# Mixer: values stored in runs of 512 bytes, first head's values loaded in the first pair, residual loaded behind the branches

## The chip, the cores and the metric

The kernel runs on one core of a Trainium2 chip. A core has TensorE (PE, matrix products), VectorE (DVE), ScalarE (ACT) and GpSimd (POOL) for element-wise work, SyncE (SP) that issues transfers, and DMA engines that move data between HBM and the on-chip memories SBUF (128 partitions) and PSUM (eight banks, where TensorE writes). Transfers are issued from SP, from ScalarE and from GpSimd; an issue stands in its engine's own order. The metric is the time of one execution in microseconds (us) on the device.

## What is computed

One layer of an encoder block on 1024 tokens of 1024 features, in float32. The part that matters here is the token mixer between two feed-forward networks:

```python
h = h + 0.5 * swiglu(rms_norm(h, ffn1_norm), ...)
u = rms_norm(h, mix_norm)
z = u @ w_in
q, k, v, s_in, gates = jnp.split(z, splits, axis=-1)          # 512, 512, 512, 512, 2048 columns
y_attn = neighbourhood_attention(q, k, v, na_rpb) @ w_attn_out  # 8 heads of 64, 16 x 64 token grid, window 8 x 16
y_ssm = s5_branch(s_in, ...) @ w_ssm_out                        # forward and backward scans of complex states, gated unit
g_attn, g_ssm = jnp.split(jax.nn.sigmoid(gates), 2, axis=-1)
h = h + (g_attn * y_attn + g_ssm * y_ssm) @ w_out
h = h + 0.5 * swiglu(rms_norm(h, ffn2_norm), ...)
...
```

The neighbourhood attention reads, for each query, keys and values of a window of 8 grid rows by 16 grid columns, adds a learned bias per head, and takes a softmax. The state-space branch scans the sequence in both directions, adds a skip term, and passes through a gated unit.

## The kernel before

Features lie on partitions, tokens along the free dimension, in two halves `t` of 512 tokens (`HT`). The normalised input of the mixer is held on chip in blocks of 128 features (`U`). Each product is done with operands split into a high and a low part, as three matmuls (`mm3`, lines 188 to 192), so that a weight block is first cast on ScalarE (`wh`, line 159) and its rest taken on VectorE (`wl`, line 160). The big products use a scheme with seven block products for a two-by-two matrix of blocks (`A7`, `ACC7`), with sums and differences of blocks made on VectorE.

The mixer has two streams of work on TensorE. The **main stream** makes the branch input (`proj`, lines 1415 to 1426), the values (`values(t)`, line 1427), and then twelve pairs of output blocks (`pairs`, line 1487: four of queries and keys, eight of gates), seven items each (`s_run`, line 1544). The weight blocks of an item are loaded from ScalarE's queue (`s_load`, line 1499) and cast some items ahead (`s_ahead`). The **side stream** is a generator (`mixer_side`, line 1312) that is advanced by `tick()`, called after every three matmuls of the main stream; a `yield n` in it means that it goes on n ticks later. In this order it does:

- `u_second`, the second half of the norm;
- sixteen injections (`inject`, line 1128): products of the branch input with small matrices, whose loads (`inject_load`, two of `fmi` and two of `ut` a pair, all from SP) run three pairs ahead; the results go into the buffer `X`;
- the scan, 128 steps on GpSimd (`scan_steps`), spread over what follows;
- attention in 64 units (8 heads, 2 row halves, 4 column blocks): scores (`attn_scores`), transposes two units later (`attn_turn`, line 1246), products with the values four units later (`attn_values`). Keys, queries, values and bias tables come from SP: `load_k` (L1203), `load_q` (L1210), `load_v` (L1215), `load_tab` (L1222). The unit order waits, as the program is written, until the first pair of query and key blocks is stored (`ready`);
- the state-space output (`ssm_out`) and the gated unit (`glu_load`, `glu_half`, lines 1272 to 1307).

Queries, keys, values, gates and both branches go through HBM, because attention reads windows of them in another layout. The values are kept as `v_d`, one row of 512 numbers for each head and grid place: four token groups of high part (64) and low part (64). `values(t)` copies each of four banks into `vh` (ScalarE) and takes `vl` (VectorE), and stores each at once from ScalarE's queue (L1449); one store writes, for 128 tokens, 64 numbers (256 bytes) into each of eight heads. The residual `h` is read back after the mixer (L1607) by sixteen loads of 256 KB from SP, into the place where `X` was.

Around it, `load_br` (lines 1451 to 1473) loads both branches, and `branches`, `gates` and `gated` multiply them with their output weights and with the gates, in four rounds of two feature blocks; `out_run` then adds the output product to the residual (L1694).

The order on TensorE is that of the program (a block of manual order). The order on the other engines is made by a planner: among the instructions that are ready by its own estimate of durations, each engine takes the one that stands first in the program; a block marked `high_priority` counts as standing 300 places earlier. Later instructions are thus put forward where an engine is free. Buffers of one tag are handed out in turn; work tiles `tmp` and weights `w` of the mixer share one tag of 24 buffers.

Of the kernel before, what the change touches and what calls it, by code (L numbers as in the profile page):

```python
# [8 lines left out]
F32 = mybir.dt.float32  # L9
# [3 lines left out]
ALU = mybir.AluOpType  # L13
# [28 lines left out]
def encoder_block(ctx, tc, I, out):  # L42
# [41 lines left out]
    def tmp(name, shape=(P, HT), dt=F32):  # L84
        return at("tmp", shape, dt, name)
# [1036 lines left out]
    def inject_load(pr):  # L1122
        fm = [ta("fmi", [P, 256]) for _ in range(2)]
        for d in range(2):
            nc.sync.dma_start(fm[d], f_d[pr, :, d * 256:(d + 1) * 256])
        return load_u(pr), fm

    def inject(pr, ut, fm):
# [62 lines left out]


    vdr = v_d.rearrange("h (r c) d -> h r c d", r=4)
    vds = v_d.rearrange("h p (g a d) -> p g a h d", g=4, a=2)
    khl, qs, vld, tabs = {}, {}, {}, {}
    late = []
    halves2 = slice(0, 64), slice(64, P)
# [114 lines left out]
    def mixer_side():  # L1312
        yield from u_second()
        while 3 not in stored:
            yield 1
        yield 7
        new_x()
        ld = {}
        for pr in range(3):
            ld[pr] = inject_load(pr)  # L1320
        yield 10
        for pr in range(NPAIR):
            if pr + 3 < NPAIR:
                ld[pr + 3] = inject_load(pr + 3)
            inject(pr, *ld.pop(pr))
            yield 2
        while 0 not in ready:
            scan_steps(1)
            yield 1
        units = [(hd, rb, cb) for hd in range(NH) for rb in range(2) for cb in range(4)]  # L1330
        n = len(units)
        load_tab(0, 0)
        load_k(0)
        load_q(0, 0)
        for cb in range(4):
            load_v(0, cb)
        for _ in range(6):
            scan_steps(1)
            yield 2
        sms, pts, O = {}, {}, {}  # L1340
        late.clear()
        lo, so = {}, {}
        for j in range(n + 5):
            if j < n:
                hd, rb, cb = units[j]
                b = 2 * hd + rb
                load_tab(b + cb // 2, (1, 2, 0, 0)[cb]) if cb < 3 else None
                if cb == 1 and rb == 0:
                    load_q(hd, 1)
                if cb == 1 and rb == 1 and hd + 1 < NH:  # L1350
                    while hd + 1 not in ready:
                        yield 1
                    load_q(hd + 1, 0)
                if rb == 0 and cb == 2 and hd + 1 in ready:
                    load_k(hd + 1)
                if rb == 1 and cb == 2 and hd + 1 < NH and hd + 1 not in khl:
                    load_k(hd + 1)
                sms[j] = attn_scores(hd, rb, cb)
            if 0 <= j - 2 < n:
                pts[j - 2] = attn_turn(units[j - 2][2], sms.pop(j - 2))  # L1360
            while late:
                nc.scalar.dma_start(*late.pop())
            if 0 <= j - 4 < n:
                hd, rb, cb = units[j - 4]
                if cb == 0:
                    O[hd, rb] = bank("O")
                attn_values(hd, rb, cb, O[hd, rb], *pts.pop(j - 4))
                if rb == 1 and hd + 1 < NH:
                    load_v(hd + 1, cb)
            scan_steps(2)  # L1370
            if j >= n:
                if j - n < 3:
                    lo[j - n] = ssm_load(j - n)
            yield 3
        scan_steps(NCH)
        for p in range(NPAIR + 1):
            if 3 <= p + 3 < NPAIR:
                lo[p + 3] = ssm_load(p + 3)
            if p < NPAIR:
                so[p] = ssm_out(p, *lo.pop(p))  # L1380
            if p > 0:
                so.pop(p - 1)()
            yield 1 + p % 2
        yield 3
        glu_load(0)
        raws = [glu_raw(0), glu_raw(1)]
        yield 11
        glu_act(0)
        glu_load(1)
        yield 2  # L1390
        glu_act(1)
        for t in range(2):
            yield from glu_half(t, raws)
# [33 lines left out]
    def values(t):  # L1427
        os_ = [bank("v") for _ in range(4)]
        for k in range(NK):
            load_wv()  # L1430
            if t == 1 and k == 0:
                s_ahead(-2)
            if t == 1 and k == 5:
                s_ahead(0)
            wh, wl = Wv[k]
            xs = U[("a11", "a12", "a21", "a22")[2 * t + k // 4]][k % 4]
            for i in range(4):
                xh, xl = (x[:, ksl(i)] for x in xs)
                T.matmul(os_[i], lhsT=xh, rhs=wh, start=(k == 0), stop=False)
                T.matmul(os_[i], lhsT=xh, rhs=wl, start=False, stop=False)  # L1440
                T.matmul(os_[i], lhsT=xl, rhs=wh, start=False, stop=(k == NK - 1))
                tick()
        for i in range(4):
            vh, vl = tmp("vh", dt=F32R), tmp("vl", dt=F32R)
            with tc.high_priority(offset=PRI):
                A.copy(vh, os_[i])
                V.tensor_tensor(vl, os_[i], vh.bitcast(F32), ALU.subtract)
            for j, x in enumerate((vh, vl)):
                nc.scalar.dma_start(vds[ksl(i % 2), 2 * t + i // 2, j], x.rearrange("p (h d) -> p h d", h=NH).bitcast(F32))  # L1449

    def load_br(t, b):

        res = []
        if b == 0:
            for k in range(0, 4, 2):
                st = tst("br")
                nc.sync.dma_start(st.rearrange("p (k c) -> p k c", k=2),
                                  o_d[k * P:(k + 2) * P, hsl(t)].rearrange("(k p) c -> p k c", p=P))
                for i in range(2):
                    hi, lo = tx("bh"), tx("bl")  # L1460
                    split(hi, lo, st[:, hsl(i)])
                    res.append((hi, lo))
            return res
        for k in range(4):
            st = tmp("br")
            hi, lo = tx("bh"), tx("bl")
            nc.sync.dma_start(st.rearrange("p (s c) -> p s c", s=L),
                              y2_d[ksl(k)].rearrange("p (s c) -> p s c", s=L)[:, :, t * 64:(t + 1) * 64])
            sv = st.rearrange("p (s c) -> p c s", s=L)
            hv, lv = (x.rearrange("p (c s) -> p c s", s=L) for x in (hi, lo))  # L1470
            split(hv, lv, sv)
            res.append((hi, lo))
        return res
# [96 lines left out]

    for t in range(2):
        values(t)
    s3s = []
    for k in range(4):
        s3 = tmp("s3")
# [26 lines left out]
    lp = ctx.enter_context(tc.tile_pool(name="lt", bufs=1, reuse_waits="tile"))  # L1602
    cur.update(tmp=(lp, "m", 17), w=(lp, "w", 20))
    h = new_h()
    for t in range(2):
        for j in range(NK):
            nc.sync.dma_start(h[j][t], h_d[:, (2 * j + t) * HT:(2 * j + t + 1) * HT])  # L1607


    def h2_block(j, t):  # L1610
# [337 lines left out]
```

## Time and profile before

| | |
|---|---|
| timed runs | 2 (2122.85 and 2125.08 us), median 2123.97 us |
| profiled execution | 2116.88 us |
| its span, first to last instruction | 2115.1 us |
| mean granted TensorE clock | 0.994 |
| TensorE busy | 2059.3 us (97%) |
| VectorE, ScalarE, GpSimd busy | 1458.8, 1010.1, 437.9 us |
| DMA packets under 512 bytes | 53472 of 225521 |

The profile is of one execution. Busy times leave out the issuing of transfers: a row with `ACTq` or `SPq` is such an issue, standing in the order of ScalarE or SP. A time in brackets is how long the engine had been idle before the row, and what ended that. "Waits" list who waited for whom; a wait for several things is put down to the one that came last. The chain of waits is followed back from the last instruction to what released each step. Some matmul records are missing from a trace, so counts in a short stretch can be a little low.

The mixer lies between about 690 and 1345 us of the span: values of the second token half and injections up to 790, the first items and the first attention units from 790 to 850, attention to 1065, state-space output to 1117, gated unit to 1172, branches from 1196 on.

### The profile page before, as it was taken

The page shows a single profiled execution, that of the slowest core. Times are in us where ns is not written, and L with a number is a line of the kernel's source. Part 1 is how long each engine was busy: PE and PEld are TensorE (multiplying, and loading weights), DVE is VectorE, ACT ScalarE, POOL GpSimd, SP SyncE. Part 2 cuts the span into 40 slices and gives each one's busy share as a digit, 9 for nine tenths or more (in the row PEclk, how much of TensorE's full clock was granted, in tenths as well). Part 3 has the DMA queues.
Part 4 walks back from the last instruction along what each step waited for, and adds up shares of the span by engine and source line. Part 5 has one row for each costly group of instructions (what it writes and reads, how often), then busy time and mean ns, then how long its engine had stood idle before and what let it go on. Part 6 is the DMA issues. An engine that isn't in the chain of part 4 may idle for free.

```text
span 2115.1 us, 28193 instructions
## 1 busy us (share of the span) xinstructions
PE 2059.3 (97%) x9518; PEld 1680.8 (79%) x9518; DVE 1458.8 (69%) x2470; ACT 1010.1 (48%) x1870; POOL 437.9 (21%) x656
## 2 busy tenths in 40 slices
PE   8999999999999997999988999999999999999998
PEld 3788888888888885788876788788888888888887
DVE  7897776667967745677644669896566565785855
ACT  6434333344445434677645546553333334545544
POOL 0037555540000518888000002000000000000000
PEclk9999999999999999999999999999999999999999
DMA  3434444485533466667677757142423338533302
GB/s 131 142 119 152 127 131 131 137 283 157 183 118 112 143 167 206 194 213 217 184 230 258 231 179 172 65 154 90 135 80 119 101 100 286 171 111 95 114 27 80
DMA packets 225521, 319.74 MB, mean 151 GB/s; under 512 B 53472, under 2 KB 93024, under 8 KB 225376
## 3 DMA queue, kind: packets, MB, share of 16 engines
q1 hardware_dynamic: 180752, 268.62, 40.0%
q10 hardware_dynamic: 42000, 44.07, 6.5%
q0 software_dynamic: 2624, 5.24, 1.3%
q8 instruction: 75, 1.23, 0.2%
q14 instruction: 70, 0.57, 0.1%
HBM read 224.01 MB, written 93.85 MB: 150 GB/s over the span
## 4 chain that ended last, share of the span: by engine, by line
PE 82%; DMA 7%; DVE 6%; ACT 2%; issue 1%; SPq 1%; ACTq 0%; DVEq 0%
PE dx L190 4%; PE dx L191 4%; PE dx L192 4%; PE gx L190 3%; PE ux L190 3%; PE gx L191 3%; PE ux L192 3%; PE ux L191 3%; PE gx L192 3%; PE dy L192 2%; PE dy L190 2%; PE dy L191 2%; PE gy L190 2%; PE uy L190 2%; PE uy L192 2%; PE gy L192 2%
## 5 line engine op out<-in xcount | busy, mean ns | idle before, releaser
L159 ACT CAST wh<-hbuf 128x512 fp32r<-128x512 f32 x280 | 172.8, 622 | 390.2 <-PE gx L191 83.5
L160 DVE TENSOR_TENSOR wl<-hbuf,wh 128x512 fp32r<-128x512 f32 x280 | 210.0, 753 | 123.9 <-ACT wh L159 121.7
L159 ACT CAST wh<-wblk 128x512 fp32r<-128x512 f32 x190 | 118.0, 622 | 193.6 <-PE dx L191 82.4
L160 DVE TENSOR_TENSOR wl<-wblk,wh 128x512 fp32r<-128x512 f32 x190 | 130.7, 690 | 50.4 <-ACT wh L159 42.9
L190 PE MATMUL dx<-ah,wh 128*128 128x512 f32 x416 | 163.5, 393 | 0.4 <-DVE hbuf L694 0.3
L192 PE MATMUL dx<-ah,wl 128*128 128x512 f32 x416 | 161.9, 389 | 0.0
L191 PE MATMUL dx<-al,wh 128*128 128x512 f32 x416 | 161.9, 389 | 0.0
L160 DVE TENSOR_TENSOR al<-araw,ah 128x512 fp32r<-128x512 f32 x154 | 106.3, 694 | 49.1 <-PE dx L191 21.1
L190 PE MATMUL gx<-xh,wh 128*128 128x512 f32 x320 | 124.9, 390 | 1.2 <-DVE c L581 1.2
L190 PE MATMUL ux<-xh,wh 128*128 128x512 f32 x320 | 124.9, 390 | 0.0
L191 PE MATMUL gx<-xl,wh 128*128 128x512 f32 x320 | 124.5, 389 | 0.0
L192 PE MATMUL ux<-xh,wl 128*128 128x512 f32 x320 | 124.5, 389 | 0.0
L192 PE MATMUL gx<-xh,wl 128*128 128x512 f32 x320 | 124.5, 389 | 0.0
L191 PE MATMUL ux<-xl,wh 128*128 128x512 f32 x320 | 124.5, 389 | 0.0
L159 ACT CAST ah<-araw 128x512 fp32r<-128x512 f32 x154 | 95.0, 619 | 43.8 <-PE dx L191 14.2
L160 DVE TENSOR_TENSOR wl<-blk,wh 128x512 fp32r<-128x512 f32 x84 | 60.8, 727 | 70.1 <-ACT wh L159 69.7
L190 PEld LDWEIGHTS dx<-ah,wh 128*128 128x128 f32 x416 | 78.1, 188 | 18.6 <-DVE hbuf L694 1.2
L428 DVE TENSOR_TENSOR hbuf<-hbuf 128x512 f32<-128x512 f32 x120 | 90.4, 754 | 2.8 <-DMA hbuf<-in_wu 0.7
L191 PEld LDWEIGHTS dx<-al,wh 128*128 128x128 f32 x416 | 78.1, 188 | 16.7 <-issue 0.7
L1156 POOL TENSOR_TENSOR sc<-X,rho 128x128 f32<-128x128 f32 x128 | 78.5, 613 | 61.6 <-ACT X L1139 51.6
L192 PEld LDWEIGHTS dx<-ah,wl 128*128 128x128 f32 x416 | 78.1, 188 | 16.3
L190 PE MATMUL px<-xh,wh 128*128 128x512 f32 x192 | 79.2, 412 | 4.3 <-ACT z L1532 3.4
(397 smaller groups left out, 5713.2 us busy)
## 6 DMA issues: line engine op xcount, KB each, us to landing
araw<-a_d SPq DMA_DIRECT2D x154, 256.0 KB
a_d<-c SPq DMA_DIRECT2D x148, 256.0 KB
wblk<-in_wd SPq DMA_DIRECT2D x88, 256.0 KB
hbuf<-in_wg SPq DMA_DIRECT2D x40, 512.0 KB
hbuf<-in_wu SPq DMA_DIRECT2D x40, 512.0 KB
blk<-in_win ACTq DMA_DIRECT2D x48, 256.0 KB
hbuf<-in_xT SPq DMA_DIRECT2D x32, 256.0 KB
h_d<-hbuf ACTq DMA_DIRECT2D x32, 256.0 KB
```

Of the source, the lines that this page charges most:

```text
L159: A.copy(hi, src)
L160: return eng.tensor_tensor(lo, src, hi.bitcast(F32), ALU.subtract)
L190: T.matmul(o, lhsT=wh, rhs=xh, start=first, stop=False, skip_group_check=more)
L191: T.matmul(o, lhsT=wh, rhs=xl, start=False, stop=False, skip_group_check=more)
L192: T.matmul(o, lhsT=wl, rhs=xh, start=False, stop=last, skip_group_check=more)
L428: V.tensor_tensor(b11, (b12, b22, None, None, b21)[i - 2], b11, ALU.subtract)
L1156: G.tensor_tensor(sc, both, rho4, ALU.mult)
```

## The change

There are four edits.

1. **Layout and stores of the values.** The rows of `v_d` are now four groups of 128 numbers, high and low part side by side as before, and a store covers both: `vs` holds, for four heads, high and low parts together. One store writes 512 bytes into each of four heads; there are again eight stores for a half, of 512 runs each instead of 1024. The copies and subtractions work on 256 columns each. The stores are not issued at once but put into the list `later`, which `s_store()` empties: for the first half in the third step of the second half's `values`, for the second half after it.
2. **Injection loads.** The second `fmi` load of a pair is issued from ScalarE instead of SP.
3. **Values of the first head.** `load_v(0, cb)` and the first table stand in the side stream right after the injections and after the last store of values, with four scan steps and four ticks before each, instead of behind the first keys and queries.
4. **Residual.** The sixteen loads of `h` are ordered behind the last load of a branch on SP.

```diff
     def inject_load(pr):
         fm = [ta("fmi", [P, 256]) for _ in range(2)]
         for d in range(2):
-            nc.sync.dma_start(fm[d], f_d[pr, :, d * 256:(d + 1) * 256])
+            (nc.sync, nc.scalar)[d].dma_start(fm[d], f_d[pr, :, d * 256:(d + 1) * 256])
         return load_u(pr), fm
...
-    vds = v_d.rearrange("h p (g a d) -> p g a h d", g=4, a=2)
+    vds = v_d.rearrange("h p (g d) -> p g h d", g=4)
...
             inject(pr, *ld.pop(pr))
             yield 2
+        while "v" not in stored:
+            scan_steps(1)
+            yield 1
+        for cb in range(4):
+            scan_steps(4)
+            yield 4
+            load_v(0, cb)
+        load_tab(0, 0)
         while 0 not in ready:
             scan_steps(1)
             yield 1
         units = [(hd, rb, cb) for hd in range(NH) for rb in range(2) for cb in range(4)]
         n = len(units)
-        load_tab(0, 0)
         load_k(0)
         load_q(0, 0)
-        for cb in range(4):
-            load_v(0, cb)
...
             if t == 1 and k == 0:
                 s_ahead(-2)
+            if t == 1 and k == 2:
+                s_store()
             if t == 1 and k == 5:
                 s_ahead(0)
...
         for i in range(4):
-            vh, vl = tmp("vh", dt=F32R), tmp("vl", dt=F32R)
-            with tc.high_priority(offset=PRI):
-                A.copy(vh, os_[i])
-                V.tensor_tensor(vl, os_[i], vh.bitcast(F32), ALU.subtract)
-            for j, x in enumerate((vh, vl)):
-                nc.scalar.dma_start(vds[ksl(i % 2), 2 * t + i // 2, j], x.rearrange("p (h d) -> p h d", h=NH).bitcast(F32))
+            for q in range(2):
+                vs = tmp("vs", [P, 4, 2, 64], F32R)
+                ov = os_[i][:, q * 256:(q + 1) * 256].rearrange("p (h d) -> p h d", h=4)
+                with tc.high_priority(offset=PRI):
+                    A.copy(vs[:, :, 0], ov)
+                    V.tensor_tensor(vs[:, :, 1], ov, vs[:, :, 0].bitcast(F32), ALU.subtract)
+                later.append((nc.scalar, vds[ksl(i % 2), 2 * t + i // 2, 4 * q:4 * q + 4],
+                              vs.rearrange("p h a d -> p h (a d)").bitcast(F32)))
...
-            nc.sync.dma_start(st.rearrange("p (s c) -> p s c", s=L),
-                              y2_d[ksl(k)].rearrange("p (s c) -> p s c", s=L)[:, :, t * 64:(t + 1) * 64])
+            mark["br"] = nc.sync.dma_start(st.rearrange("p (s c) -> p s c", s=L),
+                                           y2_d[ksl(k)].rearrange("p (s c) -> p s c", s=L)[:, :, t * 64:(t + 1) * 64]).ins
...
     for t in range(2):
         values(t)
+    s_store()
+    stored.add("v")
...
-    for t in range(2):
-        for j in range(NK):
-            nc.sync.dma_start(h[j][t], h_d[:, (2 * j + t) * HT:(2 * j + t + 1) * HT])
+    with tc.issue_after(mark["br"]):
+        for t in range(2):
+            for j in range(NK):
+                nc.sync.dma_start(h[j][t], h_d[:, (2 * j + t) * HT:(2 * j + t + 1) * HT])
```

## The prediction

> **What bounds the kernel now.** I read the head of the page first, then the waits of TensorE (engine, line, whom it waited for: total us, times, longest us).
>
> ```profile
> span 2115.1 us, 28193 instructions
> PE 2059.3 (97%) x9518; PEld 1680.8 (79%) x9518; DVE 1458.8 (69%) x2470; ACT 1010.1 (48%) x1870; POOL 437.9 (21%) x656
> ```
>
> ```profile
> PE pt L1246 <- ACT sm L1239: 15.0, 7, 7.5
> PE px L190 <- ACT z L1532: 3.4, 2, 3.2
> PE glu L190 <- ACT yh L159: 3.0, 2, 2.4
> PE inj L1132 <- DMA ut<-u_d: 2.5, 2, 2.0
> ```
>
> TensorE is busy for 2059.3 of 2115.1 us, so all its idle time is 55.8 us. The change takes no matmul away; it can only win from those 55.8 us and from matmuls that run slowly after a pause. Next I asked the timeline of TensorE for the places (start, us, line; in brackets the idle time before it and what ended it), and the chain of waits for the pace of the matmuls behind each pause (start, us, what).
>
> ```profile
> 771.61 1.32 PE L1132 MATMUL inj<-ut,fmi 128*128 128x128 f32 x8 [2.05 <-DMA ut<-u_d]
> 799.56 0.50 PE L190 MATMUL px<-xh,wh 128*128 128x512 f32 x1 [3.19 <-ACT z L1532]
> 845.97 0.90 PE L1246 MATMUL pt<-ident,sm 128*128 128x128 f32 x3 [7.49 <-ACT sm L1239]
> 1139.30 0.51 PE L190 MATMUL glu<-yh,wgl 128*128 128x512 f32 x1 [2.37 <-ACT yh L159]
> ```
>
> ```profile
> 801.98 0.43 PE px L191
> 847.72 0.43 PE px L192
> 1141.03 0.23 PE glu L190
> ```
>
> After the pauses of 3.19 and 7.49 us a 512-column matmul takes 0.43 us, after 2.37 us it takes 0.23. The twelve matmuls from 799.56 end at 804.1 instead of 802.4: 1.8 us more. Behind 845.97 about seven are slow: 1.6 us. So four places hold what the change can reach: **A**, the injections (2.5 us); **B**, the first branch products behind the values (3.19 + 1.8 = 5.0); **C**, the first attention units (7.49 + 1.6 = 9.1); **D**, the gated unit behind the scan. D comes from the windows (stretch, its length, PE busy, ..., DMA share, GB/s): PE is idle for 3.87 and 1.60 us, together 5.5.
>
> ```profile
> 1130.00:1140.00 10.00, 6.13 (x22) 3.97 (x22) 3.85 (x7) 3.52 (x8) 0.00 (x0) 1.00 1.05 395
> 1140.00:1150.00 10.00, 8.40 (x34) 6.32 (x35) 5.66 (x10) 5.28 (x10) 0.00 (x0) 1.00 0.61 207
> 1190.00:1200.00 10.00, 9.49 (x41) 7.34 (x40) 5.24 (x7) 5.97 (x8) 0.00 (x0) 1.00 0.77 207
> ```
>
> A + B + C + D = 22.1 us is the most that the change can win.
>
> What holds these places is ScalarE, and what holds ScalarE is a transfer. Its timeline, then the chain of waits at the same places:
>
> ```profile
> 762.27 0.37 ACT L1139 COPY X<-inj 64x256 f32<-64x256 f32 x1 [3.31 <-issue]
> 788.93 0.59 ACT L1446 CAST vh<-v 128x512 fp32r<-128x512 f32 x1 [7.23 <-PE v L1441]
> 797.25 1.11 ACTq L1449 DMA_DIRECT2D v_d<-vl  x1
> 798.40 0.62 ACT L159 CAST wh<-blk 128x512 fp32r<-128x512 f32 x1 [5.26 <-DMA v_d<-vh]
> 842.33 0.62 ACT L159 CAST wh<-blk 128x512 fp32r<-128x512 f32 x1 [6.95 <-DMA k_d<-qkh]
> 1138.11 0.62 ACT L159 CAST wh<-blk 128x512 fp32r<-128x512 f32 x1 [6.48 <-DMA hbuf<-h_d]
> ```
>
> ```profile
> 763.18 5.64 DMA v_d<-vl
> 768.89 2.58 DMA ut<-u_d
> 827.43 14.39 DMA vhl<-v_d
> 841.89 0.34 ACTq L1499
> 1132.25 5.36 DMA hbuf<-h_d
> 1137.71 0.35 ACTq L1499
> ```
>
> The issue on ScalarE at 841.89 loads a weight block and reads nothing of the values, yet it goes out when the value load of 827.43 has landed; so does the one at 1137.71 behind a load of the residual. So an issue here waits for some earlier, unrelated transfer, on either queue, as if transfers shared a small set of places. ScalarE works in order; its casts stand behind such an issue.
>
> **A, injections.** Eight stores of 256 bytes a run occupy ScalarE and the queues; a load of `ut` goes out at 768.89 only when the store of 763.18 has landed. The length of a store comes from two windows of the DMA queues (packets, MB, share of 16 engines): first 756 to 765 us, where q10 carries the value stores, then 816 to 842 us, where it carries mostly 2 KB runs.
>
> ```profile
> q10 hardware_dynamic: 6391, 1.61, 80.5%
> ```
>
> ```profile
> q10 hardware_dynamic: 1647, 2.99, 32.4%
> ```
>
> 0.805 x 16 x 9.0 us / 6391 = 18.1 ns for a packet of 252 bytes in the mean; 0.324 x 16 x 26 us / 1647 = 81.8 ns for 1815 bytes. No row shows 512 bytes alone; on the line between the two it is 28.7 ns (an estimate). A store had 1024 packets, 1024 x 18.1 / 16 = 1.16 us of the engines; it gets 512, 512 x 28.7 / 16 = 0.92. Eight save 1.9 us of 9.3, not half. The bounds are 18.1 ns (0.58 us a store) and twice that (no saving).
>
> The Trainium skill ("DMA: Bandwidth & Descriptors", Specifications) puts line rate at 512 bytes and more, and a read-modify-write below. Read as halving the cost, that is 0.58 us a store, 2.7 us less per eight than my estimate, and the sum below would be about 14 us instead of 11.5; no row of this trace settles it.
>
> On the other side, sixteen `fmi` loads move from SP to ScalarE, which has 3.31 us of standstill behind its own stores (row 762.27). SP gains the time of their issues; ScalarE pays 16 issues and their waits, and a load behind a burst of stores comes late. The loads run three pairs ahead, which covers them until the burst exceeds that lead. Bounds: all 2.5 us won, or 3.3 us lost once. I take 1.0 won.
>
> **B, the stores of the second half.** A half's copies on ScalarE become eight of 256 columns instead of four of 512 (VectorE's subtractions likewise); nearest rows 0.37 us (the 64x256 copy) against 0.59. Eight take 3.0 us where four took 2.4, beside matmuls. The stores were issued between the copies, the last ending at 798.36; now they are put into a list and written after all copies. From 788.93 + 3.0 = 791.9 the burst starts, about 2.4 us later than the first old issue, and saves 1.9: the cast at 798.40 would come 0.4 us later. If the planner still puts the issues between the copies, the whole 1.9 is won, the pause falls to 1.3 us, below the 2.37 that kept full pace, and 1.8 more is won: 3.7. I take 0.5, nearer the first, since the copies have the priority.
>
> The Trainium skill ("TensorE: Matmul & The Clock Gate", Part 1) has the clock halve after an idle window of about 3.4 us that runs free of the kernel. The trace agrees roughly: 3.19 us was enough, 2.37 was not; by the page's figure alone the pause at 799.56 would have cost 3.2 us, not 5.0.
>
> **C, first attention units.** The four value loads of head 0 stood on SP behind its keys and queries, and ahead of the tables for the next scores.
>
> ```profile
> 816.03 3.02 SPq L1203 DMA_DIRECT2D khl<-k_d  x4
> 825.33 2.72 SPq L1215 DMA_DIRECT2D vhl<-v_d  x4
> 1191.88 1.59 SPq L1542 DMA_DIRECT2D g_d<-z  x3
> 1199.52 4.43 SPq L182 DMA_DIRECT2D wsh<-in_was  x4
> 1204.03 6.60 SPq L1637 DMA_DIRECT2D gt<-g_d  x12
> ```
>
> They are 128 or 96 partitions of 2 KB each, 0.92 MB. Now they go out once the stores have landed, near 803 us, when SP waits for keys anyway (it moves on at 816). Their scan steps only come earlier on GpSimd, which nobody waits for there. At 839 to 842 us ScalarE then finds only small table and query transfers outstanding. It resumes at 835 instead of 842.33, the second unit's weights are ready about when TensorE reaches them at 838.5. Ends: 9.1 if the pause goes wholly; 0 if another transfer holds the same place. I take 7.0, near the upper, because the 14.39 us of the named load have no equal in that stretch.
>
> **D, gated unit.** Sixteen residual loads (256 KB each, 4.19 MB) leave this stretch; the source line's answer has their issues (count, ns, first and last start):
>
> ```profile
> L1607 SPq DMA_DIRECT2D hbuf<-h_d x16: 319/410/625, 1115.9 to 1133.0; - x16
> ```
>
> ScalarE's 6.48 us standstill loses its cause. Late next is the pair of gate-weight buffers and the vector casts, whose small pauses are part of the 5.5 us. So between 2.4 (the one pause named) and 5.5; I take 3.5.
>
> **E, where the residual goes.** The loads now follow the last branch load on SP, ahead of the weights and gates of the rows above (`wsh`, `gt`). At 395 GB/s (row 1130) they need 10.6 us, at 207 (row 1190) 20 us. SP stood idle from 1193.5 to 1199.5, so 4.6 to 14 us of delay reach the gates.
>
> ```profile
> 1196.56 0.50 PE br L191
> ```
>
> ```profile
> 1210.94 0.68 DVE L1648 TENSOR_TENSOR mg<-gt 128x512 f32<-128x512 f32 x1
> ```
>
> ```profile
> L1694 DVE TENSOR_TENSOR hbuf<-hbuf,dz x4: 677/678/679, 1289.4 to 1292.4; 128x512 f32<-128x512 f32 x4
> ```
>
> TensorE has eight groups of 12 matmuls from 1196.5, 22 us, before it needs a ninth bank at 1218.6; the first banks came free at 1210.9. So 7.6 us of delay are covered. Beyond it each us costs a us: 0 to 6.4. The residual itself is read first at 1289.4, far off. I take 0.5 lost.
>
> **Sum:** 1.0 + 0.5 + 7.0 + 3.5 - 0.5 = 11.5 us. The profiled execution took 2116.88 us (its span 2115.1 and 1.8 around it) and becomes 2105.4. It lies 7.1 us below the median of the two timed runs, 2123.97; the same gain on that gives 2112.5.
>
> **Rivals.** (1) The places are dealt anew: another transfer (a key load, a query store) holds ScalarE at C, and D's small pauses remain. For it: seven waits of that kind add up to 15.0 us in the first row of waits, only one of them C. Then A 0, B 0, C 2, D 2.4: 4.4 us, 2119.6. (2) All four places clear: 22 us, 2102; against it, D's buffers are not touched. (3) Slower: a weight-block issue on ScalarE just behind the stores shares its place with a value load. That load cannot start before the last store has landed (797.25 + 5.64 = 802.9); with the 14.39 us of the value load above it lands at 817.3, and with cast and copy TensorE resumes near 818.6 instead of 799.56: 19 us lost, against 11 won elsewhere, 2132. It decides from a landing about 6 us after 802.9. Against it: in that stretch no keys or queries stand ahead in the queue, which made the 14.39. (4) The planner puts SP's value loads where they were, and nothing at C moves: 2119.5, within (1)'s range.
>
> **How the numbers follow.** Forecast 0.52 (2107 to 2117), rival 1 0.25 (2117 to 2123), rival 2 0.10, rival 3 0.09, rival 4 0.04. From 2103 to 2124 lie the forecast, rivals 1 and 4 and half of rival 2: about 0.85, less a little since the two timed runs differ by 2.2 us themselves. About 2%, 42 us, is what a measurement of this kernel can tell from no change. To win 42 of 55.8 idle us is next to impossible: 0.01. To lose 42 takes rival 3 twice over: 0.02. The rest, 0.97, is within 2%.
>
> **What would show it.** Right: the value stores have half the packets; value loads issue on SP before the keys of head 0; no pause over 2 us at the first transposes of attention; no residual load before the branch loads, and the cast row with 6.48 us gone; TensorE still without pause from 1197 to 1290. Wrong: a longer pause at the first `px` product (B), new waits of `inj` for `fmi` (A), a pause named by `gt` or `wsh` (E), or ScalarE rows of 5 us and more ended by another transfer at C.

## The result and the profile after

The changed kernel took 2102.5 us (median of 2 runs, 2100.39 to 2104.61) against 2123.97: a ratio of 0.9899, 95% interval 0.9851 to 0.9947. That is 21.5 us where 11.5 were forecast, 0.5 us below the range of 2103 to 2124, and within 2%. Five more rounds (the first experiment) give 0.9926, 0.9904 to 0.9947: 15.4 us between the medians 2119.56 and 2104.2. Most numbers below lean on these rounds.

The profiled execution took 2100.39 us, its span is 2098.6. The head of the changed kernel's page, and its packets:

```profile
span 2098.6 us, 28228 instructions
PE 2052.0 (98%) x9518; PEld 1677.8 (80%) x9518; DVE 1460.1 (70%) x2478; ACT 1009.2 (48%) x1878; POOL 440.2 (21%) x656
DMA packets 217329, 319.74 MB, mean 152 GB/s; under 512 B 37088, under 2 KB 84832, under 8 KB 217184
```

TensorE's idle time fell from 55.8 to 46.6 us. 16384 packets under 512 bytes became 8192 of 512 or more; the bytes are the same. The waits of TensorE in the changed kernel (total us, times, longest us):

```profile
PE pt L1246 <- ACT sm L1239: 5.5, 5, 2.3
PE px L190 <- ACT z L1541: 3.4, 2, 1.8
PE br L190 <- DVE gt L1659: 3.1, 1, 3.1
PE inj L1132 <- DMA ut<-u_d: 0.2, 1, 0.2
```

The first transposes (15.0 before), the injections (2.5 before) and the gated unit's wait for `yh` (gone from the list) went as forecast. The line with `gt` is new. The same places in TensorE's timeline:

```profile
776.25 1.13 PE L1132 MATMUL inj<-ut,fmi 128*128 128x128 f32 x8 [0.24 <-DMA ut<-u_d]
795.47 0.50 PE L190 MATMUL px<-xh,wh 128*128 128x512 f32 x1 [1.76 <-ACT z L1541]
834.50 0.55 PE L1246 MATMUL pt<-ident,sm 128*128 128x128 f32 x3 [1.07 <-ACT sm L1239]
1118.74 0.50 PE L191 MATMUL glu<-yl,wgl 128*128 128x512 f32 x1 [0.91 <-DVE yl L160]
1194.69 0.50 PE L190 MATMUL br<-bh,whh 128*128 128x512 f32 x1 [3.13 <-DVE gt L1659]
```

To size the terms I took the starts of the same matmuls in two timelines and subtracted: how far the changed kernel is ahead at each, and what each stretch added (from the starts before rounding). The last columns are a second execution of it, the one profiled in the five rounds (2106.17 us).

| TensorE has come to | before, us | after, us | ahead | added | second: ahead | added | forecast |
|---|---|---|---|---|---|---|---|
| last `sin` | 729.0 | 729.4 | -0.4 | | 0.2 | | |
| last injection (A) | 779.7 | 777.1 | 2.6 | +3.0 | 3.0 | +2.8 | +1.0 |
| first scores (B) | 830.6 | 825.5 | 5.0 | +2.4 | 4.2 | +1.2 | +0.5 |
| first `O` product (C) | 850.2 | 837.5 | 12.7 | +7.7 | 12.1 | +7.9 | +7.0 |
| last `O` product | 1064.8 | 1048.4 | 16.4 | +3.6 | 10.9 | -1.2 | 0 |
| first `glu` | 1131.7 | 1117.4 | 14.2 | -2.1 | 9.9 | -1.0 | 0 |
| first `br` (D) | 1188.6 | 1168.8 | 19.8 | +5.5 | 14.9 | +5.0 | +3.5 |
| last `br` (E) | 1276.5 | 1259.9 | 16.6 | -3.2 | 10.7 | -4.1 | -0.5 |

From there to the end neither execution moves by 0.2 us against the kernel before. All five terms have the forecast's sign. A and D are well above it, E well below; they partly cancel.

### The profile page after: what moved, and what is told of

It reads as the page before. It is cut to its first block, busy times and chain, and to the rows that moved or that the text cites. A ratio compares the mean times of both kernels' runs of the same rounds, so it can differ in the third digit from the quotient of the medians.

```text
span 2098.6 us, 28228 instructions
## 1 busy us (share of the span) xinstructions
PE 2052.0 (98%) x9518; PEld 1677.8 (80%) x9518; DVE 1460.1 (70%) x2478; ACT 1009.2 (48%) x1878; POOL 440.2 (21%) x656
## 4 chain that ended last, share of the span: by engine, by line
PE 78%; DMA 10%; DVE 6%; ACT 3%; issue 1%; SPq 1%; ACTq 0%; DVEq 0%
PE dx L190 4%; PE dx L191 4%; PE dx L192 4%; PE ux L190 3%; PE ux L191 3%; PE gx L190 3%; PE ux L192 3%; PE gx L191 3%; PE gx L192 3%; DMA blk<-in_win 3%; PE dy L190 2%; PE dy L191 2%; PE dy L192 2%; DMA tb<-in_tabs 2%; PE uy L190 2%; PE gy L190 2%
## 5 line engine op out<-in xcount | busy, mean ns | idle before, releaser
L160 DVE TENSOR_TENSOR wl<-wblk,wh 128x512 fp32r<-128x512 f32 x190 | 130.4, 689 | 49.6 <-ACT wh L159 42.1
L160 DVE TENSOR_TENSOR al<-araw,ah 128x512 fp32r<-128x512 f32 x154 | 106.0, 693 | 50.7 <-PE dx L191 18.3
L159 ACT CAST ah<-araw 128x512 fp32r<-128x512 f32 x154 | 94.7, 619 | 45.9 <-PE dx L191 14.2
L192 PEld LDWEIGHTS dx<-ah,wl 128*128 128x128 f32 x416 | 78.1, 188 | 16.4
```

Source lines behind the costliest of these rows:

```text
L159: A.copy(hi, src)
L160: return eng.tensor_tensor(lo, src, hi.bitcast(F32), ALU.subtract)
L192: T.matmul(o, lhsT=wl, rhs=xh, start=False, stop=last, skip_group_check=more)
```

## The experiments

Each ratio is to the kernel before, run on the same chip beside it, with its 95% interval; 0.001 is 2.1 us. Single ratios that differ by less than about 0.002 aren't told apart by the times alone, so each verdict also names a place in the trace.

| kernel | ratio | interval |
|---|---|---|
| the whole change | 0.9926 | 0.9904 to 0.9947 |
| only the residual's move | 0.9999 | 0.9983 to 1.0014 |
| only the early value loads | 0.9985 | 0.9971 to 0.9999 |
| the same, with one unused tile | 0.9973 | 0.9964 to 0.9982 |
| only the new stores | 0.9974 | 0.9962 to 0.9986 |
| whole, `fmi` back on SP | 0.9939 | 0.9922 to 0.9957 |
| whole, runs of 256 bytes | 0.9946 | 0.9932 to 0.9960 |
| whole, stores behind all copies | 0.9961 | 0.9948 to 0.9973 |
| whole, residual back | 0.9955 | 0.9942 to 0.9967 |
| whole, value loads back | 0.9963 | 0.9952 to 0.9975 |
| whole, residual behind the first gates | 0.9911 | 0.9896 to 0.9926 |

**The whole change once more**, with no edit, in five rounds.

> The whole change once more, in five rounds. On the medians it won 21.5 us (2123.97 to 2102.5), between the two profiled executions 16.5 us (2116.88 to 2100.39). If the profiled difference is the true gain, the ratio is 0.992 (16 to 17 us); if the first medians are, it is 0.990 (21 us); by the prediction's sum it would be 0.9946 (11.5 us).

Measured 0.9926: the difference of the two profiles was the gain, and the first medians had made it too large; the interval ends just above 0.9946, the prediction's sum. The kernel before, in 56 executions beside these kernels, took 2112.84 to 2128.67 us at a mean granted clock of 0.990 to 0.996. A thousandth of clock goes with 1.6 us (a straight line through the 56): the 11 at up to 0.991 have a median of 2123.1, the 24 from 0.994 on 2117.1. The two runs from which the prediction took 2123.97 were among the slower ones.

**Parts alone.** Three kernels, each the one before with one part of the change's diff and nothing else: the residual's loads behind the last branch load, the value loads ahead of the keys, and the tiles and stores in runs of 512 bytes. Their heads:

```diff
+    with tc.issue_after(mark["br"]):
         for t in range(2):
             for j in range(NK):
```

```diff
+        while "v" not in stored:
...
+            load_v(0, cb)
+        load_tab(0, 0)
         while 0 not in ready:
```

```diff
-    vds = v_d.rearrange("h p (g a d) -> p g a h d", g=4, a=2)
+    vds = v_d.rearrange("h p (g d) -> p g h d", g=4)
...
+                later.append((nc.scalar, vds[ksl(i % 2), 2 * t + i // 2, 4 * q:4 * q + 4],
```

> Only the residual's loads are moved behind the last branch load. Theory: the gated unit alone gains D = 5 us (the 6.48 us standstill of ScalarE goes, and TensorE's pauses there go nearly to nothing), and the gates come late by E = 3.1 us (a pause of br named by gt, at the place where TensorE needs a ninth bank); sum +2 us, ratio 0.999. Rival: what the gated unit won came from the new order of the other edits; then D is 2.4 us at most, E stays, and the kernel stands still or loses 1 us, ratio 1.000.

> Only the first head's value loads are moved ahead of its keys. Theory: ScalarE's standstill of 6.95 us ahead of 842 goes, and the first transposes' pause of 7.49 us falls to about 1 us; with the slow matmuls behind it C = 7 to 8 us, and no other place of the span moves by more than 2 us; ratio 0.9965. Rival: a key or query load of head 0 takes the same place, ScalarE still stands for 4 us or more there, and the gain is 2 us; ratio 0.999.

> Only the values' tiles and stores are changed (runs of 512 bytes, issues through the list). Theory: half the packets, and the pause ahead of the first branch product falls from 3.19 to about 1.8 us and leaves no slow matmuls behind it, B = 3 us; A gives 1 to 3 us at the injections; the pause of 7.49 us at the first transposes stays. Sum 4 to 6 us, ratio 0.9975. Rival: the injections' gain belongs to the fmi loads, and only B is left, 3 us, ratio 0.9985; by the prediction's own sum B would be 0.5 us and the pause would stay over 2.4 us.

Measured 0.9999, 0.9985 and 0.9974. The residual's move won nothing: the time is the rival's number (1.000) as much as the theory's (0.999), and its interval holds both. In its profiled execution the gated unit's stretch gained 3.9 us (5 were expected) and the branch products lost 6.7 (3.1 were expected), behind the residual's own issues. The early loads won 2.3 us by the medians, of 7.4 forecast, though the place did what was said: the first `O` product came 7.7 us sooner after the first scores. In the profiled execution 5.1 us were lost again at the branch products, where the kernel before has no pause. Another 2.8 went ahead of the first scores, and 3.0 in the gated unit, where all three kernels with early loads and the residual in its old place are slow (58.7 to 61.2 us, against 56.8 to 57.7 with neither part); why was not followed up. The new stores won 4.4 us by the medians; of the stretches, A gained 0.5 and B 5.0. From the early loads' kernel, the waits of TensorE, then SP's timeline and VectorE's at the branch products:

```profile
PE pt L1246 <- ACT sm L1239: 6.0, 6, 3.0
PE br L190 <- DVE gt L1653: 3.1, 1, 3.1
```

```profile
1190.66 0.52 SPq L1472 DMA_DIRECT2D br<-y_d  x1
...
1204.66 1.76 SPq L182 DMA_DIRECT2D wsh<-in_was  x4
1206.46 8.16 SPq L1643 DMA_DIRECT2D gt<-g_d  x12
```

```profile
1196.35 8.28 DVE L160 TENSOR_TENSOR bl<-br,bh 128x512 fp32r<-128x512 f32 x8 [0.24 <-ACT bh L159]
```

No residual load is near, and still the weights go out only at 1204.66, as the last branch split on VectorE ends (1196.35 + 8.28). The memory map of the built kernels says why: the last pool lies on the memory of the one before, and here the first `wsh` falls on the buffer of the last `br` tile. In the kernel before it falls on an earlier one (1199.52), and in the whole change none of the first four does. Which tile falls where shifts with any edit. So each part alone pays at the branch products (6.7, 5.1 and 2.1 us, by the difference of `br`'s first and last start): the first to the residual's issues, the other two to such a buffer. The sum of the three stays below the whole.

**That buffer, by itself.** The early loads' kernel once more, with one unused tile at the head of the last pool:

```diff
     h = new_h()
+    V.memset(tmp("pad")[:, 0:1], 0.0)
     for t in range(2):
```

> The kernel with the early value loads alone, and one unused tile more at the head of the last pool, so that the first four weight tiles fall on buffers that no branch tile holds (in the kernel without it, the first lies where the last branch tile was, and its load went out only at 1204.66 behind the last branch split; 3.1 us of pause named by gt and 5 us lost over the branch products). Theory, buffers: the weights go out some 10 us sooner, the pause at br goes, and 4 to 5 us of the 5 come back: ratio 0.9965 against 0.9985 without the tile. Rival, queue: the weights wait for SP or for the DMA engines, the pause stays over 2.5 us, ratio 0.9985.

SP's timeline in that kernel:

```profile
1192.57 3.07 SPq L182 DMA_DIRECT2D wsh<-in_was  x4
1200.43 6.08 SPq L1644 DMA_DIRECT2D gt<-g_d  x12
```

The weights go out 12 us sooner, the pause is gone from the list, and TensorE wins 0.8 us over the branch products where it lost 5.1. The time moved less, 0.9985 to 0.9973 (2.5 us, intervals overlapping): that the buffer holds the weights is shown; its price in the time, half of what was expected, is not.

**A: which queue loads `fmi`.** The whole change with both loads on SP again:

```diff
-            (nc.sync, nc.scalar)[d].dma_start(fm[d], f_d[pr, :, d * 256:(d + 1) * 256])
+            nc.sync.dma_start(fm[d], f_d[pr, :, d * 256:(d + 1) * 256])
```

> The whole change, with all fmi loads on SP again. With the new stores alone the injections ended 0.5 us earlier than before, in the whole change 2.8. Theory: the second queue for fmi makes the other 2.3 us; without it the injections end 2.3 us later and the pause named by ut is back at 2 us; ratio 0.9937. Rival: the injections' gain is how executions differ, and nothing moves by more than 1 us; ratio 0.9926.

Measured 0.9939; the interval holds the theory's number (0.9937) and the rival's (0.9926), so the trace has to tell them apart. The waits of TensorE there:

```profile
PE inj L1132 <- DMA ut<-u_d: 2.0, 3, 0.9
```

A falls from 2.8 to 0.4 us; the pauses named by `ut` add up to 2.0 us, though none is over 0.9. Together with the stores alone (0.5) and the next kernel, in which A is 2.7 with the old runs, this settles it: A comes from the second queue, not from the halved packets.

**B: run length, and the order of the stores.** The whole change with the old tiles and runs of 256 bytes through the same list; and with the second half's stores behind the last copy (which `vc` marks):

```diff
-            for q in range(2):
-                vs = tmp("vs", [P, 4, 2, 64], F32R)
...
+            vh, vl = tmp("vh", dt=F32R), tmp("vl", dt=F32R)
...
+                later.append((nc.scalar, vds[ksl(i % 2), 2 * t + i // 2, j], x.rearrange("p (h d) -> p h d", h=NH).bitcast(F32)))
```

```diff
-    s_store()
+    with tc.issue_after(mark["vc"]):
+        s_store()
     stored.add("v")
```

> The whole change, with the old tiles and runs of 256 bytes in the stores (four copies of 512 columns, eight stores of 1024 packets), still issued through the list. Theory, run length: packets under 512 bytes are back at 53 thousand; eight stores cost 1.9 to 2.4 us more of the DMA engines, so the cast behind the burst comes that much later, the pause at the first branch product is back at 3 us or more with slow matmuls behind it, and some of the injections' gain goes: 3 to 5 us lost, ratio 0.9945. Rival, order of issue: it is the list that helps, and 1 us at most is lost; ratio 0.993.

> The whole change, with the second half's eight stores issued on ScalarE only behind the last of the eight copies, as the prediction's B had it; in the changed kernel they stand between the copies, the last is issued by 793.75 us, and the pause at the first branch product is 1.76. Theory: from about 791 on, eight issues of 0.4 to 0.9 us and the waits between them hold the cast until 796 to 798; the pause grows to 4 to 6 us with slow matmuls behind it, 3 to 5 us lost against the whole change; ratio 0.9945. Rival: the burst is over by 794 in either order, and nothing moves by more than 1 us; ratio 0.9925.

Measured 0.9946 and 0.9961. With the old runs TensorE pauses 3.31 us at the first branch product; run length and order both count, the first by the trace more than by the time, since its interval overlaps that of the whole change. ScalarE's timeline behind the copies, in the whole change, with the old runs, and with the stores last:

```profile
790.54 0.92 ACTq L1551 DMA_DIRECT2D v_d<-vs  x1
791.50 0.37 ACT L1455 CAST vs<-v 128x256 fp32r<-128x256 f32 x1 [1.18 <-DVE vs L1456]
791.58 2.17 ACTq L1551 DMA_DIRECT2D v_d<-vs  x2
793.80 0.62 ACT L159 CAST wh<-blk 128x512 fp32r<-128x512 f32 x1 [1.92 <-issue]
```

```profile
794.53 1.12 ACTq L1549 DMA_DIRECT2D v_d<-vl  x1
795.69 0.62 ACT L159 CAST wh<-blk 128x512 fp32r<-128x512 f32 x1 [5.32 <-DMA v_d<-vh]
```

```profile
791.82 0.37 ACT L1455 CAST vs<-v 128x256 fp32r<-128x256 f32 x1 [0.55 <-DVE vs L1456]
791.88 5.97 ACTq L1551 DMA_DIRECT2D v_d<-vs  x8
797.90 0.62 ACT L159 CAST wh<-blk 128x512 fp32r<-128x512 f32 x1 [5.70 <-DMA v_d<-vs]
```

In the changed kernel the stores stand between the copies and the last issue ends at 793.75; with the list emptied behind the copies eight issues take 5.97 us from 791.88, the cast comes 4.1 us later (1.1 of it from a later start of the copies), and TensorE pauses 4.76 us instead of 1.76. That is the order on which the prediction had reckoned B. It costs 7.4 us of time by the ratios, where 3 to 5 were expected, and 3.6 by the span against the second execution of the whole change; in its own place, from the last injection to the first scores, it costs 2.7 to 3.9. Where the rest of the 7.4 lies was not followed up.

**C: the early loads taken out of the whole change:**

```diff
-        while "v" not in stored:
...
         load_q(0, 0)
+        for cb in range(4):
+            load_v(0, cb)
```

> The whole change without the early value loads: the first head's values are loaded behind its keys and queries again. Theory: ScalarE stands for about 7 us ahead of the second unit of attention again, the first transposes wait 6 to 8 us with slow matmuls behind them, and C, 7 to 8 us, is lost; ratio 0.9962. Rival: with the new stores and queues the places fall otherwise there, no wait over 3 us comes back, and 2 us at most are lost; ratio 0.9935.

Measured 0.9963: 7.8 us lost, the theory's number. ScalarE's row and TensorE's in that kernel:

```profile
835.83 0.62 ACT L159 CAST wh<-blk 128x512 fp32r<-128x512 f32 x1 [6.95 <-DMA k_d<-qkh]
```

```profile
839.47 0.90 PE L1246 MATMUL pt<-ident,sm 128*128 128x128 f32 x3 [7.44 <-ACT sm L1239]
```

**What an issue waits for.** The kernel before, with the four value loads of head 0 on GpSimd's queue, no earlier than before:

```diff
-        nc.sync.dma_start(hl[0:n].rearrange("p g d -> p (g d)").bitcast(F32), vdr[hd, :, KC0[cb]:KC0[cb] + KNC[cb]])
+        (nc.sync if hd else nc.gpsimd).dma_start(hl[0:n].rearrange("p g d -> p (g d)").bitcast(F32), vdr[hd, :, KC0[cb]:KC0[cb] + KNC[cb]])
```

> The kernel before, with the first head's four value loads issued by GpSimd instead of SP, at the same place of the program and no earlier. Theory, shared places: an issue on ScalarE waits for whatever SP or ScalarE put into the same place; a load that GpSimd issues has none of these, so ScalarE's standstill of 6.95 us ahead of 842 goes or falls below 2 us, and the 7.49 us pause at the first transposes falls to 1 to 2 us. Rival: ScalarE stands because the DMA engines are full, or because the weight block itself comes late; then the standstill is within 1.5 us of 6.95. The whole time is read with care, since a slower GpSimd may cost some us elsewhere: 2110 to 2122.

GpSimd's timeline, ScalarE's, the waits of TensorE and its chain of waits (start, us, what):

```profile
830.71 2.73 POOL L1215 DMA_DIRECT2D vhl<-v_d  x4 [0.64 <-PE s L1230]
```

```profile
835.42 0.62 ACT L159 CAST wh<-blk 128x512 fp32r<-128x512 f32 x1 [0.92 <-PE s L1230]
846.36 0.59 ACT L1521 CAST qkh<-px 128x512 fp32r<-128x512 f32 x1 [5.94 <-DVE stat L1234]
```

```profile
PE pt L1246 <- ACT sm L1239: 7.0, 7, 2.8
```

```profile
834.52 9.88 DMA blk<-in_win
```

The loads go out 5 us later than on SP, and the standstill of 6.95 us ahead of the weights' cast is gone all the same; the longest pause of a transpose falls from 7.49 to 2.8 us (1 to 2 were expected). In one execution the kernel took 2113.87 us. So ScalarE was held by the places which SP's and ScalarE's transfers share, not by what the loads carry. The trace names the places: they are completion semaphores. In the kernel before, the key store issued on ScalarE at 839.30 has the semaphore of the value load that SP issued at 826.82, the weight block of 841.89 that of the value load of 827.43, and each waits for it. The rival has a part in it too: the weight block issued at 834.52 now travels for 9.88 us beside the four loads, and ScalarE stands for 5.94 us later. Loading early avoids both.

**D and E: the residual.** The whole change with its loads where they were; and with them behind the gates of the first pair (whose loads `gt` marks):

```diff
-    with tc.issue_after(mark["br"]):
-        for t in range(2):
+    for t in range(2):
```

```diff
+        if m0 == 0:
+            with tc.issue_after(mark["gt"]):
+                for t in range(2):
+                    for j in range(NK):
+                        nc.sync.dma_start(h[j][t], h_d[:, (2 * j + t) * HT:(2 * j + t + 1) * HT])
```

> The whole change without the residual's move: its loads stand in front of the gated unit again. Theory: ScalarE's standstill at the gated unit is back and D is gone, 4 to 6 us; the gates do not come sooner for it, because two of the first four weight tiles lie in buffers of the last branch tiles here (in the whole change none does), so a pause named by gt of 2 to 3 us stays. Sum 4 to 5 us lost, ratio 0.9948. Rival: the gated unit gained by the new order of its casts, not by the residual's move; then D stays, E goes, and the kernel wins 2 to 3 us more: ratio 0.9913.

> The whole change, with the residual's loads moved further, behind the first sixteen gate loads. Theory: in the changed kernel the pause of br named by gt (3.1 us, and slow matmuls of up to 1.4 us behind it) is the residual's own, whose sixteen issues hold SP from 1172.8 to 1184.8 ahead of the weights; with them behind the gates, the first weights go out before 1178 on the same scale, the pause goes, and the kernel gains another 3 to 4.5 us: ratio 0.991. The residual itself is read some 80 us after the gates' first loads, far enough for its 10 to 20 us. Rival: the weights wait for their buffers as they do in the kernels with one part each (there until the last branch split, 16 to 17 us behind the first branch product, with no residual load near), the pause stays at about 3 us, ratio 0.9926 as before.

With the residual back: 0.9955, 6.1 us lost. ScalarE's row at the gated unit:

```profile
1127.43 0.62 ACT L159 CAST wh<-blk 128x512 fp32r<-128x512 f32 x1 [6.45 <-DMA hbuf<-h_d]
```

Before it was 6.48; the standstill is the residual's. Over that stretch this kernel falls back by 1.8 us where the whole change wins 5.0 to 5.5. At the branch products it still loses 3.2 us, as much as the whole change in its first profile, with a pause of 1.8 named by `gt`: here two of the weights' buffers are late, as expected, and the weights leave SP 15.5 us behind the first branch product. SP's timeline in the changed kernel, then in the one with the residual behind the gates:

```profile
1172.82 1.42 SPq L1619 DMA_DIRECT2D hbuf<-h_d  x3
...
1178.53 6.26 SPq L1619 DMA_DIRECT2D hbuf<-h_d  x9
1185.14 2.37 SPq L182 DMA_DIRECT2D wsh<-in_was  x4
1187.85 7.77 SPq L1649 DMA_DIRECT2D gt<-g_d  x12
```

```profile
1180.83 3.20 SPq L182 DMA_DIRECT2D wsh<-in_was  x4
1184.08 6.83 SPq L1645 DMA_DIRECT2D gt<-g_d  x8
1191.01 10.97 SPq L1730 DMA_DIRECT2D hbuf<-h_d  x16
```

Against the first branch product (1168.8 and 1176.6) the weights leave 16.3 us later in the one and 4.3 in the other. The pause named by `gt` goes (0.2 us is left at `br`, for a split), and the branch products lose nothing. 0.9911 is clearly below the kernel with the residual back. Against the whole change it is 3.2 us by the ratios, within the 3 to 4.5 expected, but the intervals overlap: there the trace shows the gain, the time alone does not.

**The stretches over all fourteen profiles.** The table of terms rests on one execution of the kernel before. The same stretches, in us, in every profile of this document, split by whether the kernel has the part that bears on them:

| stretch | with the part | without it |
|---|---|---|
| A, last `sin` to last injection | 47.7 to 48.9 (7, second queue) | 50.2 and 50.3 (new stores, all loads on SP); 50.7 to 52.2 (5, neither) |
| B, to the first scores | 45.8 to 49.6 (7, runs of 512 bytes stored between the copies) | 50.3 to 53.1 (7, old runs or stores last) |
| C, to the first `O` product | 11.6 to 12.2 (9, early loads) | 19.7 to 20.8 (4); 14.9 with the loads on GpSimd's queue |
| D, first `glu` to first `br` | 51.4 to 53.0 (8, residual moved) | 56.8 to 61.2 (6) |
| E, first to last `br` | 91.1 to 94.6 (7, residual ahead of the weights) | 87.0 to 88.5 (4); 89.9 to 93.0 (3, a late buffer) |

From A to D the groups do not overlap. In E the residual and a late buffer cost about the same. The kernel before lies at or near the short end of its group in A to D, so the table of terms makes these rather too small.

## Why the prediction was wrong

The forecast, 2112.5, lay 10.0 us above the first median. 4.4 of that are the base (2123.97 against 2119.56 over 29 runs), 1.7 the first median of the changed kernel (2102.5 against 2104.2), and 3.9 the sum (15.4 measured, 11.5 forecast). By the first profile A, B, C and D gave 2.0, 1.9, 0.7 and 2.0 us more than forecast, and E 2.7 less. So what failed is the base, the sizes of A, B and D, and the cover of E. The prediction noted that its profiled execution lay 7.1 us below the median and then worked from the median; it allowed for the 2.2 us between its two runs, on a kernel whose executions spread by 16. That rival 2's number (2102) came up is luck: the base and the first median made 6.1 us of it, B kept a pause of 1.76 and E lost 3.2.

**A** failed in size, for the wrong reason. The step put the gain mainly on shorter stores and set it against `fmi` waiting behind them on ScalarE: 1.0. Shorter stores alone gave 0.5, no more than kernels without the part differ among themselves; the second queue gave 2.4, and no wait of `inj` for `fmi` came up. The upper bound of 2.5 would have been the better value.

**B** failed in its premise, that "they are put into a list and written after all copies", with the burst from 791.9. A list in program order is no order on the engine: the planner issued each store as its tile was ready. The prediction's other branch came true, a pause "below the 2.37 that kept full pace" (1.76), with 2.4 and 1.2 us won instead of that branch's 3.7. The size of a store was right: from the DMA answer for 787 to 797 us of the changed kernel,

```profile
q10 hardware_dynamic: 4079, 2.03, 72.9%
```

0.729 x 16 x 10 us / 4079 = 28.6 ns a packet of 498 bytes in the mean, against the estimate of 28.7. The Trainium skill ("DMA: Bandwidth & Descriptors", Specifications) has line rate from 512 bytes on; read as half the cost of a store, that does not hold here: 28.6 ns against 18.1 makes 0.92 us against 1.16.

**C** was right: 7.7 and 7.9 us for 7.0, and the mechanism is shown both ways, by taking the loads back and by moving them to another queue without making them earlier. Rival 1, another transfer in the same place, did not come; nor did rival 3: on SP in the changed kernel

```profile
796.41 2.67 SPq L1215 DMA_DIRECT2D vhl<-v_d  x4
```

the value loads went out when the cast they might have held (793.80) had run.

**D** was right in its cause and low in size: 5.5 and 5.0 for 3.5, at or near its upper bound of 5.5. The small pauses taken for what is "late next" went with the large one.

**E** is the step that failed most: -3.2 and -4.1 for -0.5. The queue was foreseen, the pause named by `gt` was on the list of what would show it wrong, and the delay came out at the low end of its 4.6 to 14 us: counted from the first branch product, the weights leave SP after 16.3 us instead of 10.9, and the first product with a gate starts after 25.1 us instead of 20.2. The cover was wrong. The prediction let the eight groups of matmuls begin at 1196.5, which is a later row of the chain ("branches from 1196 on" in the account of the profile before is the same slip); the first branch product stands at 1188.60, and the ninth group (`whh`) begins at 1211.41, not at 1218.6. TensorE's timeline and VectorE's in the kernel before, then VectorE's in the changed kernel:

```profile
1188.60 0.39 PE L190 MATMUL br<-bh,wh 128*128 128x512 f32 x1
1211.41 0.39 PE L190 MATMUL br<-bh,whh 128*128 128x512 f32 x1
```

```profile
1208.76 0.69 DVE L1647 TENSOR_TENSOR gt<-br,gt 128x512 f32<-128x512 f32 x1
```

```profile
1193.94 2.11 DVE L1659 TENSOR_TENSOR gt<-br,gt 128x512 f32<-128x512 f32 x3
```

The first product with a gate reads the first bank and so frees it, at 1208.76 + 0.69 = 1209.45. The cover was 1211.41 - 1209.45 = 2.0 us, not 7.6, and a delay of 4.9 leaves 2.9 of pause; it measured 3.13. In the second execution 3.4 us at half the clock follow the pause. The prediction also took SP's idle time up to 1199.52 for slack. SP was not idle but waiting for a buffer of a branch split; in the changed kernel that buffer was free, and the residual's loads took its place as the thing waited for.

## What to carry to other kernels

A cover counted in matmuls begins at the first of them: look that up by its tile, since the chain of waits passes over most of a stage. Before you count an idle queue as slack, ask what its next issue waits for: a buffer there can be the real limit, and any edit that shifts the rotation moves it. Bulk loads with a far deadline belong behind every load with a near one, not merely out of the way of the stage that suffers now. Forecast from the middle of many executions or say how far they spread: here two runs were off by as much as a whole term of the sum.

## What the runs showed of the hardware

**The clock can fall after the pause is over.** The same pause in two executions of the same kernel, from the two timelines and the windows of 795 to 800 us (the last three columns are the granted clock, the DMA share and GB/s); first the execution whose row at 795.47 stands above:

```profile
795.00:800.00 5.00, 4.53 (x20) 3.77 (x21) 4.90 (x8) 4.61 (x9) 4.53 (x7) 1.00 0.73 235
```

Then the second execution's window, and its timeline (the first row has the pause):

```profile
795.00:800.00 5.00, 4.86 (x14) 3.86 (x15) 4.89 (x7) 3.75 (x9) 4.47 (x7) 0.66 0.66 225
```

```profile
795.14 0.50 PE L190 MATMUL px<-xh,wh 128*128 128x512 f32 x1 [1.80 <-ACT z L1541]
795.47 0.39 PE L191 MATMUL px<-xl,wh 128*128 128x512 f32 x1
...
796.62 0.62 PE L190 MATMUL px<-xh,wh 128*128 128x512 f32 x1
797.04 0.63 PE L191 MATMUL px<-xl,wh 128*128 128x512 f32 x1
...
800.03 0.40 PE L192 MATMUL py<-xh,wl 128*128 128x512 f32 x1
```

1.76 us left the clock at 1.00; 1.80 us brought it down, 1.5 us after the matmuls had started again, from 796.62 to 800.03: 3.4 us at half pace, 1.6 us lost. In the kernel before it also fell late, at 800.93, 1.4 us behind the pause of 3.19. The Trainium skill ("TensorE: Matmul & The Clock Gate", Part 1) has the clock judged in windows of about 3.4 us that run free of the kernel. The length agrees, and so does the chance in it; but the page asks for an idle window of that length, and here 1.80 us of pause was enough. The clock's record in the traces says more. In the fourteen profiles, between its first rise and its last fall, the clock fell 53 times, always at a boundary of a grid of 3.413 us that is fixed within an execution, and for one to three of its steps. TensorE had been idle, in all, for at least 1.63 us of the step before (with the profile's modelled ends of matmuls). Every step at full clock with over 1.93 us of idle time was followed by a fall, none with under 1.63 was, and between these it went both ways. Of the two pauses above, the boundary at 793.94 cut the one of 1.76 us in 0.23 and 1.53; the one of 1.80 lay in one step. So it was luck of the grid that 2.37 us kept the clock in the kernel before (1.93 of it lay in one step), and the pause's length alone is no bound. It also bears on the table above: `O`'s stretch, +3.6 in one execution and -1.2 in the other, is no term of the change. It ran at half the clock for 6.8 us in the kernel before, for 3.4 in the first execution and 6.8 in the second, so 1.7 us of the +3.6 are clock and nothing of the -1.2; the rest are small waits that were not followed up.

**Transfers on SP and ScalarE share places, GpSimd's do not.** An issue on ScalarE stood 6.95 us for a load on SP with which it shares no data (in the kernel before, and with the early loads taken out of the whole change); with the load on GpSimd's queue that wait was gone. In the traces of the mixer the issues on SP and ScalarE carry eight semaphores between them (99, 101, 103 to 107 and 109), those on GpSimd others (from 111 on). The numbers are given out when the program is built, so this is a property of the built program, and not of the queues.
